# Spreading 32 DRAM-to-DRAM weight-sum transfers along the weight stream of an SSD and GLA kernel

## Chip, cores and metric

The kernel runs on one core of one Trainium2 chip. The metric is the device time of one execution in microseconds (us), as the median of several runs. The engines are TensorE (PE, with its weight loads shown apart as PEld), VectorE (DVE), ScalarE (ACT), GpSimd (POOL) and SyncE (SP); DMAs are issued from the queues of SP and POOL and run on the core's 16 DMA engines.

## The reference

Two layers of a residual network act on x of 512 tokens by 1024 features, each behind an RMS norm, with a last RMS norm at the end.

```
h = x
h = h + ssd_mixer(rmsnorm(h), ...)     # layer 1: 32 heads in 8 groups, scanned in both directions
h = h + gla_mixer(rmsnorm(h), ...)     # layer 2: 4 heads
return rmsnorm(h, final_norm)

def gla_mixer(u, w_in, ...):
    q, k, v, z, gl = split(u @ w_in)   # v and z: 4 heads of 512 columns each
    ...                                # decay from gl, attention in both directions, norm, times silu(z)
    return o @ w_out
```

The products are wanted in float32. Each weight is split into a high and a low part, and each product is made of three matmuls.

## The kernel before, in words

**The weight stream.** All weights go through one object, `Weights` (L46 to L113). A list of 146 specs names the tiles of 512 KB in the order of their use; `W.pos` counts the one in use. `W.next()` is called where the matmuls of a position are written. It splits ahead to position `pos + 2`, loads ahead to `pos + 2`, and hands out the parts. A load goes from SP's queue into one of three `wraw` buffers (L65). The split is a cast on ACT into `whi` (L85, or L90 in two halves where a column scale applies) and a subtraction on DVE into `wlo` (L86 or L91); there are three buffers of each. `W.mark` is the ACT instruction of the latest split. Positions 0 to 64 belong to the SSD layer (`n1` in the diff is 65), 65 to 145 to the GLA layer. A position is 24 matmuls, or 12 in the block products of GLA (`block_mm`, L801).

**The SSD layer.** The loop over g (L727) projects group g and runs the scan of group g - 1 in between, a part at each call of `step()` (L731). `scan_group` asks for two tiles `bct` of 1 MB from DRAM on POOL's queue (`load_bc`, L533); there are two buffers, which come free with the matmuls of `outputs` (L652). ACT adds biases to `bct` (L611), DVE selects (L616), ACT takes exponentials (L619), DVE multiplies (L620), PE multiplies (L652). Then `y` is gated (L662), squared on ACT (L666), its root taken on POOL (L303, L304), scaled on ACT (L669), and transposed on PE into `pty` (L677).

**The weight sums.** GLA's v and z of a head are computed with seven block products (`vz_part`) in place of eight, for which four sums w1 to w4 of blocks of `w_in` are needed. For each of the 4 heads `Blocks.step(n)` (L249) starts transfer n of 8 from DRAM to DRAM on POOL's queue, 1 MB each: n = 0, 1, 4 and 6 are copies (L264), n = 2, 3, 5 and 7 accumulate (L262), here called adds. Within a head n = 2 follows on n = 0, 3 on 1, 4 on 2, 5 on 4, 6 on 5 and 7 on 6. Each waits for `W.mark` by a manual dependency:

```
tc.add_manual_dep(dma.ins, W.mark.ins.name, ..., reason="pace")
```

The sums are read back as `wraw<-wsumw` at positions of the head's `vz_part`: from 72 for head 0, 88 for head 1, 108 for head 2, 128 for head 3. Before the change the list is ordered by n and then by head (L278), and each `step()` of the SSD loop with g of 1 or more starts the next (L732), so all 32 are started in groups 1 to 5.

**Order.** The instructions are ordered on each engine by a list scheduler that works with priorities and modelled times; an engine's queue then runs in that order, POOL's and SP's too. Tail parts at the end are ordered by hand (`manual_schedule`, L1094).

Of the kernel before, what the change touches and what calls it, by code (L numbers as in the profile page):

```python
# [45 lines left out]
class Weights:  # L46
    def __init__(self, tc, pool):
        self.tc, self.nc, self.pool = tc, tc.nc, pool
        self.specs = []
        self.alt = {}  # L50
        self.raw = {}
        self.spl = {}
        self.pos = 0
        self.n_raw = 0
        self.n_spl = 0

# [44 lines left out]
    def next(self):  # L101
        n = len(self.specs)
        while self.n_spl < n and self.n_spl <= self.pos + LOOK_SPL:
            while self.n_raw <= self.n_spl:
                self._load(self.n_raw)
                self.n_raw += 1
            with self.tc.high_priority(offset=SPLIT_AHEAD):
                self._split(self.n_spl)
            self.n_spl += 1
        self.load_ahead()  # L110
        i = self.pos
        self.pos += 1
        return self.spl.pop(i)  # L113


def build(tc, I, out):
    nc = tc.nc
    ctx = ExitStack()
    with ctx:
# [3 lines left out]
        W = Weights(tc, cp)  # L123
# [90 lines left out]
        def outw(w, r0, scale):  # L214
            for hf in range(2):
                for kk in range(2):
                    W.add(
                        w[r0 + kk * 256 : r0 + (kk + 1) * 256, hf * 512 : (hf + 1) * 512].rearrange(
                            "(k p) f -> p k f", p=P
                        ),  # L220
                        (2, 512),
                        scale=scale[:, kk * 2 : kk * 2 + 2],
                    )
# [14 lines left out]
        last1 = len(W.specs) - 1  # L238

        class Blocks:  # L240
# [8 lines left out]
            def step(self, n):  # L249
                w = self.w  # L250
                dst, src, add = (
                    (w["w1"], self.b11, False),
                    (w["w3"], self.b12, False),
                    (w["w1"], self.b12, True),
                    (w["w3"], self.b22, True),
                    (w["w2"], w["w1"], False),
                    (w["w2"], self.b22, True),
                    (w["w4"], w["w2"], False),
                    (w["w4"], self.b21, True),
                )[n]  # L260
                if add:
                    dma = nc.gpsimd.dma_start(dst, src, accum_op=ALU.add)  # L262
                else:
                    dma = nc.gpsimd.dma_start(dst, src)  # L264
                tc.add_manual_dep(
                    dma.ins, W.mark.ins.name,
                    mybir.DependencyInfo(mybir.DependencyClass.Sync, mybir.DependencyReason.DATA),
                    reason="pace",
                )
# [5 lines left out]
                        W.add(src[kk * 256 : (kk + 1) * 256].rearrange("(k p) f -> p k f", p=P), (2, 512))  # L275

        blocks = [Blocks(hd) for hd in range(GH)]
        sums = [(b, n) for n in range(8) for b in blocks]  # L278

        def qk_specs(hd):  # L280
            chan(w_in2, GQ0 + hd * P)
            chan(w_in2, GK0 + hd * P)
# [8 lines left out]
        for hd in range(GH):  # L291
# [3 lines left out]
            if hd + 1 < GH:  # L295
                qk_specs(hd + 1)
        outw(w_out2, 3 * 512, onT)

        uh = cp.tile([P, KD, L], F32R, name="uh")
        ul = cp.tile([P, KD, L], F32R, name="ul")  # L300
# [32 lines left out]
        def proj_tok(step=lambda: None):  # L333
            pts = [mmb(f"ptk{t}") for t in range(NT)]
            for kk in range(4):
                if kk:
                    step()
                wh, wl = W.next()
                for t in range(NT):
                    sl = slice(t * P, (t + 1) * P)  # L340
                    for j in range(2):
                        k = 2 * kk + j
                        mm3(pts[t], (uh[:, k, sl], ul[:, k, sl]), (wh[j], wl[j]), k == 0, k == KD - 1)
            return pts

        def proj_out(yts, step=lambda: None):
            for hf in range(2):
                pts = [mmb(f"po{t}") for t in range(NT)]
                for kk in range(2):
                    if hf or kk:  # L350
                        step()
                    wh, wl = W.next()
                    for t in range(NT):
                        for j in range(2):
                            k = 2 * kk + j
                            mm3(pts[t], yts(k, t), (wh[j], wl[j]), k == 0, k == 3)
                for t in range(NT):
                    hs = h[t][:, hf * 512 : (hf + 1) * 512]
                    nc.vector.tensor_tensor(out=hs, in0=hs, in1=pts[t], op=ALU.add)  # L359
# [27 lines left out]
        with tc.tile_pool(name="sp", bufs=1, reuse_waits="tile") as sp:  # L387
# [108 lines left out]
            def proj_group(g, step):  # L496
                b = conv_silu(proj_ch(), 16 + g, "bch")
                step()
                c = conv_silu(proj_ch(), 24 + g, "cch")
                step()  # L500
                x0 = conv_silu(proj_ch(), 2 * g, "xch")
                step()
                x1 = conv_silu(proj_ch(), 2 * g + 1, "xch")
                return b, c, x0, x1

            def z_gate(pts, pool, n):
                zs = []
                for t in range(NT):
                    if t % 2 == 0:
                        zs.append(pool.tile([P, 2, 512], F32, tag="zs", name=f"zs{t}", bufs=n))  # L510
                    z = zs[-1][:, t % 2]
                    nc.scalar.activation(z, pts[t], AF.Tanh, scale=0.5)
                    nc.vector.scalar_tensor_tensor(
                        out=z, in0=z, scalar=1.0, in1=pts[t], op0=ALU.add, op1=ALU.mult
                    )
                return zs
# [193 lines left out]
            def yts1(pr):  # L710
                def f(k, t):
                    yh, yl = yT[2 * pr + k // 2]
                    sl = slice(t * P, (t + 1) * P)
                    return yh[:, k % 2, sl], yl[:, k % 2, sl]

                return f
# [10 lines left out]
            for g in range(G + 1):  # L727
                it = iter(scan_group(g - 1, grp.pop(g - 1), zs[(g - 1) // 2])) if g else iter(())
                left = [SCAN_STEPS, 4 * ((g % 2 == 0 and g < G) + (g < G) + (g in (3, 5, 8)))]

                def step():  # L731
                    if g and sums:  # L732
                        b, i = sums.pop(0)
                        b.step(i)
                    n = -(-left[0] // max(left[1], 1))
                    left[0] -= n
                    left[1] -= 1
                    for _ in range(n):
                        next(it, None)

                if g < G:
                    if g % 2 == 0:
                        zs[g // 2] = z_gate(proj_tok(step), sp, 3)
                        step()
                    if g == 0:
                        dt_part()
                    grp[g] = proj_group(g, step)
                    step()
                if g in (3, 5, 8):
                    proj_out(yts1(g // 2 - 1 if g < 8 else 2), step)  # L750
                for _ in it:
                    pass
# [366 lines left out]
```

## Time and profile before

| what | value |
|---|---|
| median of 3 runs | 894.0 us (893.67 to 896.81) |
| the profiled execution | 896.26 us |
| its span, first to last instruction | 894.6 us |
| mean granted TensorE clock | 0.986 of full speed |
| PE busy | 847.1 us (95%) |
| DVE, ACT, POOL busy | 678.3, 512.7, 99.8 us |
| moved by DMA | 132.92 MB |

All times within the program are counted from the span's start. A row of a timeline gives start, duration and instruction, and in brackets the idle time of the engine before it and what ended it. A DMA's time to landing counts from its issue. What an engine is not kept from doing by another is busy time; only idle time of PE, and time at a lower PE clock, can be won without removing matmuls.

### The profile page before, as it was taken

How to read it: one execution, taken by the hardware profiler on the slowest of the kernel's cores; microseconds unless marked ns; L12 is line 12 of the kernel's file. 1: busy time of each engine (PE TensorE's matmuls, PEld its weight loads, DVE VectorE, ACT ScalarE, POOL GpSimd, SP SyncE). 2: the span in 40 equal slices, each digit the busy share in tenths (PEclk: the TensorE clock that was granted, in tenths of full speed). 3: DMA queues.
4: the chain of work that ended last, by engine and by line, in shares of the span. 5: the costliest groups of instructions: out<-in, count | busy, mean ns of one | idle time of the engine just before them, and what ended most of it. 6: DMA issues, size and time to landing. Idle time of an engine off the chain costs nothing.

```text
span 894.6 us, 11289 instructions
## 1 busy us (share of the span) xinstructions
PE 847.1 (95%) x3976; PEld 691.9 (77%) x3976; DVE 678.3 (76%) x1040; ACT 512.7 (57%) x1082; POOL 99.8 (11%) x172
## 2 busy tenths in 40 slices
PE   7999989979999999999898998999999999999996
PEld 5777778868887788888777776877887788778875
DVE  6398968789658987679698689878855886588653
ACT  6338478556546746567485548586525652575333
POOL 2002022111111110000001140000001000100012
PEclk9999999989999999999899999999999999999999
DMA  7337659998799794332222135513532363236202
GB/s 252 95 97 288 209 195 225 259 185 279 203 252 341 180 214 140 95 109 103 95 95 94 42 104 164 144 46 125 182 95 71 118 189 91 75 102 213 85 1 94
DMA packets 90198, 132.92 MB, mean 149 GB/s; under 512 B 7969, under 2 KB 49149, under 8 KB 87966
## 3 DMA queue, kind: packets, MB, share of 16 engines
q1 hardware_dynamic: 76412, 80.68, 30.0%
q0 software_dynamic: 13728, 51.52, 21.0%
q8 instruction: 31, 0.51, 0.2%
q14 instruction: 25, 0.20, 0.1%
q10 hardware_dynamic: 2, 0.00, 0.0%
HBM read 129.96 MB, written 35.78 MB: 185 GB/s over the span
## 4 chain that ended last, share of the span: by engine, by line
PE 60%; DVE 12%; ACT 10%; issue 7%; DMA 7%; POOL 3%; POOLq 0%; SPq 0%; ACTq 0%; DVEq 0%
DMA bct<-cumd 5%; PE pb L137 4%; PE pb L138 4%; PE pb L139 4%; PE pch L138 4%; PE pch L139 4%; PE pch L137 4%; PE po L137 4%; PE po L138 4%; PE po L139 4%; DVE wlo L86 2%; PE pyi L652 2%; PE ptk L139 2%; PE ptk L137 2%; PE ptk L138 2%
## 5 line engine op out<-in xcount | busy, mean ns | idle before, releaser
L85 ACT CAST whi<-wraw 128x1024 fp32r<-128x1024 f32 (+1 forms) x114 | 118.8, 1043 | 140.4 <-PE pb L139 40.5
L86 DVE TENSOR_TENSOR wlo<-wraw,whi 128x1024 fp32r<-128x1024 f32 (+1 forms) x114 | 140.4, 1233 | 76.9 <-ACT whi L85 76.5
L138 PE MATMUL pch<-ul,whi 128*128 128x512 f32 (+2 forms) x336 | 134.0, 399 | 0.0
L139 PE MATMUL pch<-uh,wlo 128*128 128x512 f32 (+2 forms) x336 | 133.3, 397 | 0.6 <-DVE wlo L86 0.5
L137 PE MATMUL pch<-uh,whi 128*128 128x512 f32 (+2 forms) x336 | 133.7, 398 | 0.0
L139 PEld LDWEIGHTS pch<-uh,wlo 128*128 128x128 f32 (+2 forms) x336 | 62.9, 187 | 15.1 <-DVE wlo L86 1.5
L137 PEld LDWEIGHTS pch<-uh,whi 128*128 128x128 f32 (+2 forms) x336 | 62.8, 187 | 13.9 <-issue 0.2
L138 PEld LDWEIGHTS pch<-ul,whi 128*128 128x128 f32 (+2 forms) x336 | 62.8, 187 | 13.9 <-issue 0.5
L488 DVE SCALAR_TENSOR_TENSOR cv<-pch,colA,cv 128x511 f32<-128x511 f32 (+1 forms) x96 | 70.9, 743 | 0.4
L90 ACT ACTIVATE whi<-wraw,colB 128x512 fp32r<-128x512 f32 x58 | 38.8, 716 | 44.5 <-PE pch L138 20.1
L611 ACT ACTIVATE bct<-bct,eb 128x128 f32<-128x128 f32 x128 | 41.5, 392 | 22.8 <-DMA bct<-cumd 19.5
L137 PE MATMUL ptk<-whi,uh 128*128 128x512 f32 x128 | 51.3, 403 | 0.0
L303 POOL TENSOR_SCALAR rs<-ss 128x2 f32<-128x2 f32 (+1 forms) x32 | 8.0, 250 | 386.7 <-ACT gy L1025 309.5
L139 PE MATMUL ptk<-whi,ul 128*128 128x512 f32 x128 | 50.8, 398 | 0.0
L138 PE MATMUL ptk<-wlo,uh 128*128 128x512 f32 x128 | 50.8, 397 | 0.0
L91 DVE SCALAR_TENSOR_TENSOR wlo<-wraw,colB,whi 128x512 fp32r<-128x512 f32 x58 | 41.7, 748 | 9.2 <-ACT whi L90 8.7
L619 ACT ACTIVATE bct<-bct,eb 128x128 f32<-128x128 f32 x128 | 41.3, 392 | 6.1 <-DVE bct L616 6.0
L137 PE MATMUL pb<-whi,uh 128*128 128x512 f32 x96 | 38.6, 402 | 2.0 <-DVE u L825 2.0
L137 PE MATMUL po<-whi,yh 128*128 128x512 f32 x96 | 38.7, 406 | 0.0
L138 PE MATMUL pb<-wlo,uh 128*128 128x512 f32 x96 | 38.6, 403 | 0.0
L359 DVE TENSOR_TENSOR h<-h,po 128x512 f32<-128x512 f32 x48 | 31.9, 683 | 8.8 <-PE po L139 8.7
L138 PE MATMUL po<-wlo,yh 128*128 128x512 f32 x96 | 38.4, 400 | 0.0
(306 smaller groups left out, 2050.1 us busy)
## 6 DMA issues: line engine op xcount, KB each, us to landing
wraw<-in_ssd_w_in_dram SPq DMA_DIRECT2D x48, 512.0 KB, 6.8
wsumw<-in_gla_w_in_dram POOLq DMA_DIRECT2D x24, 1024.0 KB, 11.0
bct<-cumd POOLq DMA_DIRECT2D x16, 1024.0 KB, 7.7
wraw<-in_gla_w_in_dram SPq DMA_DIRECT2D x32, 512.0 KB, 3.7
wraw<-wsumw SPq DMA_DIRECT2D x32, 512.0 KB, 3.5
wraw<-in_ssd_w_out_dram SPq DMA_DIRECT2D x16, 512.0 KB, 5.1
wraw<-in_gla_w_out_dram SPq DMA_DIRECT2D x16, 512.0 KB, 3.8
h<-in_x_dram SPq DMA_DIRECT2D x4, 512.0 KB, 6.5
```

Source lines behind the costliest of these rows:

```text
L85: self.mark = nc.scalar.copy(vh, raw)
L86: nc.vector.tensor_tensor(out=vl, in0=raw, in1=vh.bitcast(F32), op=ALU.subtract)
L90: self.mark = nc.scalar.mul(hs[j], raw[:, j], g)
L91: nc.vector.scalar_tensor_tensor(out=ls[j], in0=raw[:, j], scalar=g, in1=hs[j].bitcast(F32), op0=ALU.mult, op1=ALU.subtract)
L137: nc.tensor.matmul(pt, lhsT=a[0], rhs=b[0], start=first, stop=False)
L138: nc.tensor.matmul(pt, lhsT=a[0], rhs=b[1], start=False, stop=False)
L139: nc.tensor.matmul(pt, lhsT=a[1], rhs=b[0], start=False, stop=last)
L359: nc.vector.tensor_tensor(out=hs, in0=hs, in1=pts[t], op=ALU.add)
L488: nc.vector.scalar_tensor_tensor(out=cv[:, o0:o1], in0=pt[:, o0 + s : o1 + s], scalar=cwt(j, a), in1=cv[:, o0:o1], op0=ALU.mult, op1=ALU.add,)
L611: nc.scalar.activation(bct[:, r], bct[:, r], AF.Identity, bias=TM["eb"][:, cc, i : i + 1])
L619: nc.scalar.activation(et[:, r], et[:, r], AF.Exp, bias=TM["eb"][:, cc, i : i + 1])
L652: nc.tensor.matmul(py[:, q * 256 + r * 64 : q * 256 + (r + 1) * 64], lhsT=et[:, r], rhs=xt[:, cc, r * 64 : (r + 1) * 64], start=True, stop ...
```

## The change

The list of sums and its use in `step()` go. `W.next()` looks up its position in a table `W.beside` and runs what it finds, after the splits and loads ahead have been asked for. The table holds the 32 transfers, head by head and n = 0 to 7 within a head: 20 at positions 8, 10, 13, 16, 19, 21, 24, 27, 30, 32, 35, 38, 41, 43, 46, 49, 52, 54, 57 and 60 of the SSD layer, and 12 at positions 68, 73, 78, 83, 88, 92, 96, 100, 104, 108, 112 and 116, within the first three heads of GLA. So heads 0 and 1 are complete by position 49; the first four transfers of head 2 are at 52 to 60, its last four at 68 to 83; head 3 is at 88 to 116. The transfers, their sizes, queue and kind of wait are the same.

```
         self.pos = 0
+        self.beside = {}
...
         self.load_ahead()
         i = self.pos
+        self.beside.get(i, lambda: None)()
         self.pos += 1
...
         blocks = [Blocks(hd) for hd in range(GH)]
-        sums = [(b, n) for n in range(8) for b in blocks]
...
+        n1 = last1 + 1
+        at = [8 + (n1 - 10) * i // 20 for i in range(20)] + [n1 + i for i in (3, 8, 13, 18, 23, 27, 31, 35, 39, 43, 47, 51)]
+        for i, pos in enumerate(at):
+            W.beside[pos] = lambda b=blocks[i // 8], n=i % 8: b.step(n)
...
                 def step():
-                    if g and sums:
-                        b, i = sums.pop(0)
-                        b.step(i)
```

## Rows read from the trace of the kernel before

**Rows 1.** The page, busy time of each engine.
```profile
PE 847.1 (95%) x3976; PEld 691.9 (77%) x3976; DVE 678.3 (76%) x1040; ACT 512.7 (57%) x1082; POOL 99.8 (11%) x172
```

**Rows 2.** Busy time by stretch; the last three columns: PE clock, DMA share, GB/s.
```profile
69.00:190.00 121.00, 109.94 (x533) 91.06 (x534) 99.80 (x175) 83.89 (x216) 20.64 (x30) 0.96 0.84 238
190.00:335.00 145.00, 142.03 (x687) 117.72 (x687) 116.42 (x188) 84.94 (x208) 21.55 (x32) 1.00 0.90 236
335.00:428.00 93.00, 92.62 (x463) 77.28 (x462) 73.24 (x121) 59.27 (x146) 4.51 (x9) 1.00 0.35 109
428.00:500.00 72.00, 63.95 (x319) 52.94 (x318) 56.39 (x99) 43.04 (x120) 7.43 (x16) 0.95 0.27 88
```

**Rows 3.** DMA issues in 60 to 340 us: count, KB each, median us to landing.
```profile
wraw<-in_ssd_w_in_dram SPq DMA_DIRECT2D x28, 512.0 KB, 9.2
bct<-cumd POOLq DMA_DIRECT2D x11, 1024.0 KB, 8.9
```

**Rows 4.** DMA issues in 340 to 500 us.
```profile
bct<-cumd POOLq DMA_DIRECT2D x5, 1024.0 KB, 5.6
```

**Rows 5.** Timeline of PE, instructions that it came late to, 110 to 442 us.
```profile
112.98 0.48 PE L677 MATMUL pty<-idn,y 128*128 128x128 f32 x1 [2.76 <-ACT y L669]
...
182.53 0.98 PE L548 MATMUL ptx<-idn,cv 128*128 128x128 f32 x7 [3.33 <-DVE cv L493]
...
185.26 1.12 PE L553 MATMUL ptb<-idn,cv 128*128 128x128 f32 x4 [1.50 <-ACT xt L549]
...
285.32 0.70 PE L635 MATMUL pti<-st,cv 128*128 128x256 f32 x2 [1.31 <-DVE t L642]
...
303.50 0.66 PE L553 MATMUL ptb<-idn,cv 128*128 128x128 f32 x4 [0.93 <-ACT xt L549]
...
440.97 0.47 PE L677 MATMUL pty<-idn,y 128*128 128x128 f32 x1 [2.90 <-ACT y L669]
```

**Rows 6.** Busy time by stretch, as in group 2, around one stall.
```profile
179.00:192.00 13.00, 8.16 (x32) 6.33 (x31) 11.79 (x26) 8.30 (x19) 1.82 (x2) 0.74 1.10 233
```

**Rows 7.** Timeline of ACT, 155 to 438 us.
```profile
169.66 1.05 ACT L85 CAST whi<-wraw 128x1024 fp32r<-128x1024 f32 x1 [3.87 <-DMA wraw<-in_ssd_w_in_dram]
...
174.40 1.87 ACT L611 ACTIVATE bct<-bct,eb 128x128 f32<-128x128 f32 x6 [3.01 <-DMA bct<-cumd]
...
432.44 1.34 ACT L90 ACTIVATE whi<-wraw,colB 128x512 fp32r<-128x512 f32 x2 [6.55 <-PE pch L138]
...
437.81 0.69 ACT L611 ACTIVATE bct<-bct,eb 128x128 f32<-128x128 f32 x2 [3.37 <-DVE bct L616]
```

**Rows 8.** The chain that ended last, two loads on it: start, us.
```profile
102.49 7.50 DMA bct<-cumd
...
163.23 11.14 DMA bct<-cumd
```

**Rows 9.** DMA issues in 429.5 to 430 us.
```profile
bct<-cumd POOLq DMA_DIRECT2D x1, 1024.0 KB, 8.1
```

**Rows 10.** DMA issues in 312.5 to 316 us, a stream load beside one add.
```profile
wraw<-in_ssd_w_in_dram SPq DMA_DIRECT2D x1, 512.0 KB, 9.3
```

**Rows 11.** DMA issues in 204 to 205.5 us, a stream load beside one copy.
```profile
wraw<-in_ssd_w_in_dram SPq DMA_DIRECT2D x1, 512.0 KB, 6.8
```

**Rows 12.** DMA issues in 500 to 890 us.
```profile
wraw<-wsumw SPq DMA_DIRECT2D x32, 512.0 KB, 3.5
```

**Rows 13.** Timeline of ACT in the GLA layer.
```profile
545.12 1.06 ACT L85 CAST whi<-wraw 128x1024 fp32r<-128x1024 f32 x1
...
551.96 1.04 ACT L85 CAST whi<-wraw 128x1024 fp32r<-128x1024 f32 x1
...
627.05 1.05 ACT L85 CAST whi<-wraw 128x1024 fp32r<-128x1024 f32 x1 [1.67 <-PE pb L139]
```

**Rows 14.** Timeline of DVE in the GLA layer.
```profile
554.86 1.22 DVE L86 TENSOR_TENSOR wlo<-wraw,whi 128x1024 fp32r<-128x1024 f32 x1
...
628.14 1.23 DVE L86 TENSOR_TENSOR wlo<-wraw,whi 128x1024 fp32r<-128x1024 f32 x1 [1.50 <-ACT whi L85]
```

## Prediction, made before the change was run

> **What bounds the kernel now.** I read the page first: PE is busy for 847.1 us [rows 1], so matmuls set the time, and only the 47 us in which PE is idle, and the time at half clock, are open to a change that moves no matmul. Next comes the table by stretch [rows 2]. From 69 to 335 us, where all 32 transfers run, PE is idle for 121 - 109.94 + 145 - 142.03 = 14.0 us, and the DMA engines are 84 to 90% busy. From 335 to 428 us the same loop goes on with no transfer in it: PE is idle for 0.4 us, DMA is at 35%. From 428 us the scan of the last group has little left to cover it, and PE is idle for 8.1 us with no transfer near. The reader should see that crowding of DMA and idle PE stand together, but that the last stretch has a cause of its own.
>
> The DMA tables say what crowding costs a load: among the transfers a stream load lands after 9.2 us and a bct tile after 8.9 [rows 3]; later bct takes 5.6 [rows 4] and a stream load in GLA 3.5 [rows 12].
>
> Then the timelines, for how a late load reaches PE. Six waits make up 12.7 us, over half of the idle PE time between 69 and 500 us [rows 5]. Before the one at 182.53 us ACT sat idle twice, 3.87 us for a stream load and 3.01 us for a bct tile [rows 7], and the chain shows that tile landing 11.14 us after its issue [rows 8]. ACT runs in order, so the convolution work behind the tile came late, then DVE's, then PE's. The clock also fell: 0.74 over 13 us [rows 6] is 0.26 x 13 = 3.4 us lost between the full level and half. The stall at 112.98 has the same form: a bct tile issued at 102.49 lands at 109.99 [rows 8], and the squares of y stand behind it on ACT.
>
> **The change, part by part.** Nothing is removed: 32 issues of the same size stay on POOL, which is busy 11% [rows 1]. What changes is what each transfer runs beside. I placed the new transfers in the old time scale by the casts of ACT, one per position: a transfer at position p waits for the cast of p + 2. Some anchors: 23 is cast at 169.66 us, 59 at 432.44 [rows 7], 75 at 545.12 [rows 13]. In the SSD layer one transfer then starts about every 20 us (20 over some 400 us), where before there were 32 in about 260, one every 8.
>
> *Middle of SSD.* By this placement (an estimate) the transfers near 163 us are a copy at about 152 and an add at about 171, and the tile issued at 163.23 meets neither in full. In the old order, with one start every 8 us and landings of some 11, adds overlapped there all the time. I take the stall at 182.53 and 185.26 as gone: 3.33 + 1.50 [rows 5] + 3.4 of clock [rows 6] = 8.2 us. The two small waits at 285.32 and 303.50 follow on crowded loads too: 1.31 + 0.93 [rows 5] = 2.2 us gone. At 97 us an add now stands where a copy stood, and the tile of 102.49 still meets it: its 7.50 [rows 8] goes towards 8.9 [rows 3], so I add 1 us to that stall. Other waits I leave as they are. Part sum: -8.2 - 2.2 + 1.0 = -9.4 us. Bounds: nothing, if DVE (74 to 82% busy here, from [rows 2]) holds PE anyway; at most all 14.0 us idle and 0.04 x 121 = 4.8 us of clock [rows 2], -18.8.
>
> *End of SSD.* Four transfers now fall behind 380 us. The add at position 57 waits for the cast of 432.44 (until 433.8) [rows 7]; the tile issued at about 429.7 lands 8.1 us later [rows 9], at 437.8, when ACT goes on [rows 7], and PE waits 2.90 us at 440.97 [rows 5]. Beside an add that tile goes from 8.1 towards the 11.14 of a crowded one [rows 8]: 0 to 3.0 us, straight into the stall. I take +2. The add at position 60 comes near 459 us; the loads then are ahead of need, +0.
>
> POOL's queue runs in order, so what stands behind a waiting transfer matters: the bct issues, the roots of L303 and L304, and in GLA the same roots for the gate. Each transfer waits for a cast that comes two positions before use, so the wait seldom outlasts what is behind it. If the add of position 57 were ordered ahead of the tile of 429.7, the tile would leave about 4.5 us later (cast end 433.8, about 0.4 us more to issue); I keep this as an upper end.
>
> *GLA.* Twelve transfers are added to a layer that had none. A position here lasts 1.05 + 1.67 = 2.72 us [rows 13]. ACT's cast waits for PE (the split buffers), and the load three positions on leaves when DVE has split: 628.14 + 1.23 - 627.05 = 2.3 us after the cast starts [rows 13, 14]. A load thus has 3 x 2.72 - 2.3 = 5.9 us until its cast is due, and takes 3.5 [rows 12]: 2.4 us spare. A late cast in turn has 2 x 2.72 - 2.3 = 3.1 us before PE misses it. So an isolated load may take 5.9 + 3.1 = 9.0 us. Beside one copy a load took 6.8 us [rows 11]: hidden, +0, unless several follow each other. Beside one add it took 9.3 [rows 10]: 0.3 us too much, and the load after it stands in the same queue. I take 0.5 us for each of the adds at 96, 108 and 116: +1.5; bounds 0 and 9.3 - 5.9 = 3.4 each, if no split buffer is ahead.
>
> Head 0 is tighter. The add of position 73 leaves after the cast that ends at 546.2 [rows 13]. The load cast at 551.96 left about 547.5 (the split of three positions earlier); beside the add it lands near 556.8, cast end 557.8, where DVE wanted it at 554.86 [rows 14]: 2.9 us late on an engine that has no idle time there. I take 2.5; bounds 0 and 2.9. The adds of 83 and 100 fall where positions are twice as long: +0. The first transfer of this part, at 68, meets no tight load: +0.
>
> **Sum.** -9.4 + 2.0 + 1.5 + 2.5 = -3.4 us. The profiled execution took 896.26 us, 1.7 around its span of 894.6: 892.9 on its scale. It lies 2.3 above the median of 894.0, so on the median I forecast 890.6. Measurement of this kernel can tell about 0.5%, 4.5 us, from no change; the forecast lies just inside.
>
> **The rivals.**
>
> 1. *The sum above*: the middle of SSD is freed, the tail and GLA give about two thirds back. 890.6; own range 886 to 895. Chance 0.48 (0.19 of it faster, 0.29 the same).
>
> 2. *Nothing is given back.* The split buffers hide every add, the tail's tile lands before the add has moved much: 894.0 - 9.4 = 884.6, and down to 894.0 - 18.8 = 875 if all idle time of the stretch goes. For it: the load tolerance of 9.0 us is nearly what a load beside an add takes. Against: head 0 has no such reserve. Chance 0.20, faster.
>
> 3. *The spreading frees nothing.* A tile meets a transfer in the new places as often as not, and each stall is DVE's in the end: middle of SSD 0, the other terms +6: 894 to 900. For it: DVE is 74 to 82% busy, and the stall's own release is DVE's [rows 5]. Against: 93 us without transfers and without idle PE [rows 2]. Chance 0.16 (0.12 the same, 0.04 slower).
>
> 4. *Slower: GLA's weight stream falls behind.* Three raw buffers give 2.4 us spare; four adds in block products (73, 96, 108, 116) at the full 3.4 us, and four copies (78, 88, 92, 112) at 6.8 - 5.9 = 0.9 us, come to 17.2. With the tail and the SSD gain: 894.0 - 9.4 + 2.0 + 17.2 = 903.8. It decides from where GLA loses 9.4 - 2.0 + 4.5 = 11.9 us, seven tenths of that. For it: 9.3 against 3.5 us [rows 10, 12]. Against: the split buffers. Chance 0.16 (0.15 slower, 0.01 the same). The Trainium skill, in "DMA: Bandwidth & Descriptors", section "Issuing engines are not separate DMA queues", says that DMAs of all issuing engines share the same 16 DMA engines and interleave; by that rule a transfer on POOL's queue slows SP's loads wherever it is put, and the trace agrees in size, 9.3 against 3.5 us.
>
> That the change starts fewer or other transfers is excluded: the table has 32.
>
> **How the numbers follow.** Faster 0.19 + 0.20 = 0.39; the same 0.29 + 0.12 + 0.01 = 0.42; slower 0.04 + 0.15 = 0.19. The range leaves out the far half of rivals 2 and 4: 881 to 902.
>
> **What would show it.** Right: from 130 to 335 us PE idle under 2 us and no half clock near 185; bct tiles at 6 to 7.5 us in the median; the last bct tile but one at 10 us and a longer wait before `pty` in the tail; a longer PE wait in head 0's block products; stream loads of 7 to 9 us in GLA beside adds, with PE waits under 1 us. Wrong: stalls of the 182 kind that come back elsewhere in SSD (rival 3), or casts in GLA that wait for DMA for several us (rival 4); or a scheduler that orders ACT, DVE or POOL anew because modelled transfer times moved.

## The result: slower by 0.9%, and where the time went

The changed kernel takes 900.68 us in the median (900.16 to 904.0, 4 runs), against 894.37 for the kernel before, run beside it: a ratio on record of 1.0093, 95% interval 1.0065 to 1.0121; the two medians alone give 1.0071. The forecast was a small gain, 890.6; measured is a loss, 6.3 us by the medians. The profiled execution took 900.56 us with a span of 898.9, so the two profiled spans differ by 4.3 us, and the time can be placed by them. Lines of the code have moved down by 1 to 6: L677 of before is L683 after, L85 is L86, L359 is L365, L262 is L264.

The table by stretch, the changed kernel, columns as in [rows 2]:

```profile
69.00:190.00 121.00, 113.72 (x560) 95.10 (x561) 103.44 (x181) 87.37 (x225) 12.39 (x20) 0.97 0.56 161
190.00:335.00 145.00, 144.12 (x711) 120.17 (x710) 118.34 (x192) 87.43 (x218) 15.35 (x24) 1.00 0.61 170
335.00:428.00 93.00, 92.34 (x457) 77.13 (x456) 75.43 (x127) 55.31 (x132) 9.06 (x14) 1.00 0.54 161
428.00:500.00 72.00, 59.62 (x291) 48.74 (x289) 49.45 (x87) 43.62 (x123) 8.91 (x19) 0.93 0.36 94
500.00:890.00 390.00, 371.32 (x1685) 301.77 (x1686) 282.65 (x391) 204.64 (x327) 43.16 (x63) 0.99 0.49 141
```

Against [rows 2] the DMA share of the first two stretches falls from 0.84 and 0.90 to 0.56 and 0.61, and PE idles 121 - 113.72 + 145 - 144.12 = 8.2 us there in place of 14.0. The loads there land sooner, DMA issues in 60 to 340 us as in [rows 3]:

```profile
wraw<-in_ssd_w_in_dram SPq DMA_DIRECT2D x30, 512.0 KB, 5.4
bct<-cumd POOLq DMA_DIRECT2D x12, 1024.0 KB, 7.4
```

So the middle of the SSD layer was relieved. From 428 to 500 us PE idles 12.4 us in place of 8.1. Over 500 to 890 us PE is busy for 371.32; the same stretch of the kernel before reads

```profile
500.00:890.00 390.00, 375.69 (x1710) 305.24 (x1708) 286.03 (x396) 208.78 (x336) 35.77 (x57) 1.00 0.36 109
```

To place the loss I compare the start of the same PE instruction in both. PE's timeline before, for instructions that [rows 5] lacks:

```profile
129.22 0.33 PE L677 MATMUL pty<-idn,y 128*128 128x128 f32 x1 [1.44 <-ACT y L669]
...
478.51 0.50 PE L137 MATMUL pr<-thw,yh 128*128 128x512 f32 x1 [1.91 <-DVE h L359]
...
497.19 0.66 PE L321 MATMUL ptn<-idn,xn 128*128 128x128 f32 x4 [0.60 <-DVE ul L143]
...
690.41 0.66 PE L1013 MATMUL ptyg<-idn,gy 128*128 128x128 f32 x4 [0.76 <-DVE gy L1027]
...
781.25 0.66 PE L1013 MATMUL ptyg<-idn,gy 128*128 128x128 f32 x4 [0.76 <-DVE gy L1027]
```

and the same instructions after, with the one long wait in head 0 (559.39) between them:

```profile
113.50 0.47 PE L683 MATMUL pty<-idn,y 128*128 128x128 f32 x1 [5.63 <-ACT y L675]
130.73 0.33 PE L683 MATMUL pty<-idn,y 128*128 128x128 f32 x1 [1.65 <-ACT y L675]
...
431.09 0.33 PE L683 MATMUL pty<-idn,y 128*128 128x128 f32 x1 [2.40 <-ACT y L675]
...
471.76 0.80 PE L139 MATMUL pr<-thw,yh 128*128 128x512 f32 x1 [6.79 <-DVE h L365]
...
492.93 0.66 PE L327 MATMUL ptn<-idn,xn 128*128 128x128 f32 x4 [1.18 <-DVE ul L145]
...
559.39 0.77 PE L139 MATMUL pb<-whi,uh 128*128 128x512 f32 x1 [5.83 <-DVE u L828]
...
691.67 0.55 PE L1016 MATMUL ptyg<-idn,gy 128*128 128x128 f32 x3 [0.76 <-DVE gy L1030]
...
785.59 0.66 PE L1016 MATMUL ptyg<-idn,gy 128*128 128x128 f32 x4 [0.76 <-DVE gy L1030]
```

The wait of 112.98 in [rows 5] begins at 112.98 - 2.76 = 110.22, after at 113.50 - 5.63 = 107.87: 2.4 us gained up to there. By 130.73 (129.22 before) 1.5 us are lost: the stall between cost 3.9. By the wait of 431.09 (440.97 in [rows 5]; both less their wait, 428.69 and 438.07) 9.4 us are gained. By 492.93 it is 4.3: the tail gave back 5.1. By 691.67 there is a loss of 1.3: head 0 cost 5.5 (head 1 hardly adds). By 785.59 it is 4.3: head 2 cost 3.1. Nothing more follows; 4.3 is the difference of the spans.

**The stall at 113 us.** DMA issues of POOL in 95 to 100.5 us, after:

```profile
wsumw<-in_gla_w_in_dram POOLq DMA_DIRECT2D x1, 1024.0 KB, 11.8
bct<-cumd POOLq DMA_DIRECT2D x1, 1024.0 KB, 9.9
```

The add at position 13 stands where a copy stood, as foretold. The tile behind it lands after 9.9 us in place of 7.50 [rows 8], and PE waits 5.63 in place of 2.76.

**The tail.** The add of position 60 leaves POOL at 458.39 us, and SP issues the next stream load 0.8 us later. Timelines of POOL, ACT and DVE there, and under them the chain of waits:

```profile
458.39 1.12 POOL L264 DMA_DIRECT2D wsumw<-in_gla_w_in_dram  x1 [11.26 <-ACT whi L91]
...
467.61 1.04 ACT L86 CAST whi<-wraw 128x1024 fp32r<-128x1024 f32 x1 [7.39 <-DMA wraw<-in_gla_w_in_dram]
...
468.68 1.23 DVE L87 TENSOR_TENSOR wlo<-wraw,whi 128x1024 fp32r<-128x1024 f32 x1 [3.83 <-ACT whi L86]
```
```profile
459.18 8.35 DMA wraw<-in_gla_w_in_dram
```

The load brings position 65, the first weights of the GLA layer, which PE uses much later. But its split stands in ACT's and DVE's order ahead of work of the tail: `h` (L365) is behind `wlo` (L87) on DVE, and the PE wait of 471.76 is for `h`. The kernel before had three of its four `h` behind that split too (DVE: `wlo` at 475.43, `h` from 477.78). So a load of which PE has no need yet holds up PE through two queues.

**Head 0.** The add of position 73 leaves at 543.08. Timelines of ACT and DVE, then the chain:

```profile
553.73 1.04 ACT L86 CAST whi<-wraw 128x1024 fp32r<-128x1024 f32 x1 [5.16 <-DMA wraw<-wsumw]
...
554.81 1.23 DVE L87 TENSOR_TENSOR wlo<-wraw,whi 128x1024 fp32r<-128x1024 f32 x1 [3.36 <-ACT whi L86]
```
```profile
546.91 9.33 DMA wraw<-wsumw
```

Two loads in a row are late beside one add: the first lands for the cast of 553.73, and DVE, which had no idle time at this point before [rows 14], stands 3.36 us. The second, issued at 546.91, takes 9.33 us, and the chain runs through it to `u` (L828) and to the PE wait of 559.39.

**The clock.** Three stretches of the changed kernel after its long waits, columns as in [rows 2]:

```profile
108.00:118.00 10.00, 4.50 (x13) 3.67 (x14) 5.06 (x9) 7.31 (x25) 0.91 (x2) 0.66 0.07 22
...
469.00:478.00 9.00, 6.24 (x27) 5.26 (x28) 5.84 (x9) 5.83 (x21) 0.90 (x2) 0.62 0.41 133
556.00:566.00 10.00, 6.61 (x18) 5.29 (x19) 7.76 (x14) 5.05 (x8) 0.52 (x1) 0.66 0.81 244
```

Each of the three waits of 5.6 to 6.8 us is followed by time at half clock: 0.34 x 10 or 0.38 x 9 = 3.4 us lost between the full level and half. Before, the first and the last of these places read 0.83 over 10 us (1.7 lost), and the one in the tail 1.00.

### The profile page after: what moved, and what is told of

Read it like the earlier page. It is cut to its first block, busy times and chain, and to the rows that moved or that the text cites. A ratio compares the mean times of both kernels' runs of the same rounds, so it can differ in the third digit from the quotient of the medians.

```text
span 898.9 us, 11292 instructions
## 1 busy us (share of the span) xinstructions
PE 845.4 (94%) x3976; PEld 691.1 (77%) x3976; DVE 677.8 (75%) x1040; ACT 513.1 (57%) x1082; POOL 100.8 (11%) x172
## 4 chain that ended last, share of the span: by engine, by line
PE 29%; DVE 7%; ACT 5%; DMA 5%; issue 2%; POOL 2%; POOLq 0%; SPq 0%; ACTq 0%; DVEq 0%
PE pb L139 3%; PE pb L140 3%; PE pb L141 3%; PE po L141 2%; PE po L139 2%; PE po L140 2%; DMA wraw<-wsumw 2%; DMA wraw<-in_gla_w_in_dram 2%; DVE wlo L87 1%; PE pch L140 1%; PE pch L139 1%; PE pch L141 1%; ACT whi L86 1%; PE pr L141 1%; PE pr L140 1%
## 5 line engine op out<-in xcount | busy, mean ns | idle before, releaser
L87 DVE TENSOR_TENSOR wlo<-wraw,whi 128x1024 fp32r<-128x1024 f32 (+1 forms) x114 | 140.4, 1234 | 86.1 <-ACT whi L86 85.7
L86 ACT CAST whi<-wraw 128x1024 fp32r<-128x1024 f32 (+1 forms) x114 | 118.8, 1043 | 149.8 <-PE pch L140 42.3
L139 PEld LDWEIGHTS pch<-uh,whi 128*128 128x128 f32 (+2 forms) x336 | 62.5, 186 | 13.6
L365 DVE TENSOR_TENSOR h<-h,po 128x512 f32<-128x512 f32 x48 | 32.0, 683 | 9.0 <-PE po L141 9.0
L141 PE MATMUL pb<-whi,ul 128*128 128x512 f32 x96 | 38.4, 400 | 0.0
L141 PE MATMUL po<-whi,yl 128*128 128x512 f32 x96 | 38.1, 397 | 0.0
## 6 DMA issues: line engine op xcount, KB each, us to landing
wsumw<-in_gla_w_in_dram POOLq DMA_DIRECT2D x24, 1024.0 KB, 10.4
```

The costliest lines, as they stand in the source:

```text
L86: self.mark = nc.scalar.copy(vh, raw)
L87: nc.vector.tensor_tensor(out=vl, in0=raw, in1=vh.bitcast(F32), op=ALU.subtract)
L139: nc.tensor.matmul(pt, lhsT=a[0], rhs=b[0], start=first, stop=False)
L141: nc.tensor.matmul(pt, lhsT=a[1], rhs=b[0], start=False, stop=last)
```

## The experiments

Ratios are to the kernel before, run on the same chip, with 95% intervals, as they stand on record; they need not be the quotients of the medians, and a difference of two ratios is known to 0.3 to 0.6%. Sizes in us are such differences times 894. In experiments 1 to 4 and 7 to 10 the traces show PE's matmuls in the changed kernel's order. In the diffs only the places in the list `at` are shown. "GLA transfers" are the twelve at positions 68 to 116.

**1. No transfers in GLA.** The last 12 transfers are left out, and the loads of the sums that are then missing (two of head 2, all four of head 3) read a weight block instead.

```
-        for i, pos in enumerate(at):
+        for i, pos in enumerate(at[:20]):
```

> This kernel leaves out the 12 transfers of the GLA layer; loads of head 2 (w2, w4) and of head 3 (w1 to w4) read a block of the weights instead, so the loads are as many and as large. The instruction order on PE, DVE, ACT is the changed kernel's. Theory (adds beside loads that are due just in time cost the GLA layer about 9 us: 6 in head 0, 3 in head 2): 900.7 - 9 = 891.7 us, ratio to before 0.997, and the PE wait at 553.6 us falls from 5.7 to about 2 us. Rival (the GLA loss is something that the SSD part carries over, such as order or an earlier start): 899 to 901, the PE wait stays over 5 us.

Measured: 888.16 us, 0.9941 (0.9921 to 0.9961). The GLA half of the change costs 1.0093 - 0.9941 = 1.5%, 13.6 us, so the SSD half alone is a gain. That is more than the 9 us expected and than the 8.6 that the trace places in heads 0 and 2. The tail's wait stays, 7.02 us at 469.62; that of head 0 falls to 2.02.

**2. The tail's add alone moved.**

```
-... 54, 57, 60, 68, 73, ...
+... 54, 57, 82, 68, 73, ...
```

> One transfer moved: the add of position 60 goes to position 82, between GLA heads 0 and 1, where the next load has some 20 us in hand. Theory (that add stands in front of the first GLA load, whose cast holds up ACT and DVE in order at 460 to 468 us): 900.7 - 4.6 = 896 us, ratio to before 1.002, the PE wait of 6.8 us near 465 falls to about 2 us and the load of position 65 lands in 4 us instead of 8.4. Rival (the tail is slower because its instruction order changed): 900 to 901, the wait stays over 5 us, since the order is kept but for two instructions.

Measured: 896.27 us, 1.0042 (1.002 to 1.0065): 0.5%, 4.6 us, from one transfer (the interval touches that of the changed kernel, so the size is rough). The wait for `h` falls to 2.88 us; that of head 0 stays, 6.12.

**3. The GLA transfers moved.** All twelve run, at other positions, outside the block products.

```
-... 68, 73, 78, 83, 88, 92, 96, 100, 104, 108, 112, 116
+... 68, 82, 84, 98, 100, 102, 103, 105, 118, 119, 121, 123
```

> All 12 GLA transfers stay in GLA but move from the block products to the stretches of query, key and output products between heads: positions 68, 82, 84, 98 (head 2) and 100, 102, 103, 105, 118, 119, 121, 123 (head 3). Theory (place, not number, costs): the GLA loss of 9 us goes as when they are left out, 892 us, ratio 0.997. Rival (12 MB more traffic in GLA costs wherever it runs): 897 to 901.

Measured: 889.43 us, 0.9965 (0.9946 to 0.9985). PE's timeline at head 0, where the wait of 5.83 stood:

```profile
554.47 0.47 PE L139 MATMUL pb<-whi,uh 128*128 128x512 f32 x1 [0.54 <-DVE u L828]
```

The same twelve transfers cost nearly nothing here: 0.9965 against 0.9941 without them, which is inside the noise. What costs is the place; by this experiment the old places cost 1.0093 - 0.9965 = 1.3%, 11.4 us.

**4. Both, and position 13 moved to 12.** The moves of 2 and 3 together (here 60 goes to 83), and the add ahead of the tile of the 113 us stall one position earlier.

```
-... 10, 13, 16, ... 57, 60, 68, 73, ...
+... 10, 12, 16, ... 57, 83, 68, 82, ...
```

> The GLA places of the third kernel, the add of position 60 at 83, and the add of position 13 at 12, so that it starts some 9 us earlier and is done before the bct tile of about 100 us is asked for. Theory: 900.7 - 9 (GLA) - 4.6 (tail) - 4 (the 5.6 us wait and half clock near 108 us) = 883 us, ratio 0.988; the wait near 108 us falls to 1.5 us or less. Rival (that early wait is DVE's, not the tile's): 887, the wait stays over 4 us.

Measured: 881.82 us, 0.9872 (0.985 to 0.9893), faster than both kernels: by 1.3% than before, by 2.2% than the change. PE's timeline at the three places:

```profile
109.88 0.33 PE L683 MATMUL pty<-idn,y 128*128 128x128 f32 x1 [1.90 <-ACT y L675]
...
461.98 0.77 PE L139 MATMUL pr<-thw,yh 128*128 128x512 f32 x1 [2.88 <-DVE h L365]
...
545.65 0.47 PE L139 MATMUL pb<-whi,uh 128*128 128x512 f32 x1 [2.05 <-DVE u L828]
```

The waits of 5.63, 6.79 and 5.83 us are back at 1.9 to 2.9. Of the 2.2%, experiment 2 explains 0.5 and experiment 3 1.3; the 0.4 that are left, 3.8 us, are the size of the stall at 113 (3.9 above). That move was not run by itself, but up to this point in time no other transfer has been moved, and the wait there is 3.7 us shorter.

**5 and 6. The transfers nearly without traffic**, in the old order and in the new: each transfer moves 16 of its 512 rows, and the loads of the sums read a weight block.

```
+                dst, src = dst[0:16], src[0:16]
```

> The kernel before, with each of the 32 transfers cut to its first 16 of 512 rows (32 KB in place of 1 MB), and the weight loads of the sums reading a block of the weights instead. The instruction order of PE, DVE, ACT is exactly that of before. Theory (before the change, traffic of the transfers cost what PE lost between 69 and 335 us): the 14.0 us of idle PE there fall to 4 or less and the half clocks there go; 12 to 16 us faster than before, ratio 0.983 to 0.987. Rival (those waits are DVE's or the order's): 1 to 5 us faster, ratio 0.995 to 0.999.

Measured, kernel before cut in this way: 880.46 us, 0.9871 (0.9833 to 0.991). Between 69 and 335 us PE still idles 7.0 us, more than the 4 expected.

> The changed kernel, cut in the same way; its instruction order of PE, DVE, ACT is exactly the changed kernel's. Theory (order is worth little, traffic all): within 3 us of the fifth kernel, ratio to before 0.982 to 0.988, which makes the changed kernel's transfers cost about 20 us where they stand and those of before about 14. Rival (part of the loss is the new order): slower than the fifth kernel by 4 us or more, ratio over 0.989.

Measured, changed kernel cut in this way: 881.2 us, 0.9888 (0.9839 to 0.9936). In both the instructions stand in the order of the full kernel. So the two orders are worth the same within the noise, and the difference is the traffic: it cost 1.3% in the old places and 1.0093 - 0.9888 = 2.0% in the new. The profiled spans agree: 894.6 - 881.1 = 13.5 us in the old, 898.9 - 880.2 = 18.7 in the new. Experiment 4, at 0.9872 with all its traffic and a span of 879.5, pays about nothing for it.

**7. Head 0's places alone.**

```
-... 60, 68, 73, 78, 83, 88, ...
+... 60, 68, 82, 83, 84, 88, ...
```

> The changed kernel with head 0's three transfers moved behind its block products: 73 to 82, 78 to 83, 83 to 84; the other nine of GLA stay. Theory: the wait of 5.7 us and the half clock near 553 us go, 6 us of the changed kernel's loss: ratio to before 1.002 to 1.004. Rival (the transfers in the block products of heads 1 and 2 carry most of the GLA loss): ratio 1.006 to 1.009.

Measured: 895.35 us, 1.0041 (1.0011 to 1.0071), 0.5% or 4.6 us from head 0, with intervals that overlap; its wait is 2.03.

**8. One add put back at 73** into experiment 3.

```
-... 60, 68, 82, 84, 98, ...
+... 60, 68, 73, 84, 98, ...
```

> The third kernel (GLA transfers between the heads), with one add put back from position 82 to 73, within head 0's block products. Theory: the PE wait near 550 us comes back at about 5.7 us with 6.8 us at half clock: 6 us slower than the third kernel, ratio to before about 1.003. Rival (one transfer is absorbed, only a row of them costs): 0 to 2 us, ratio 0.997 to 0.999.

Measured: 895.51 us, 1.0037 (1.0013 to 1.0061): 0.7%, 6.4 us, for one transfer in this place. DMA issues around it, and PE's timeline:

```profile
wsumw<-in_gla_w_in_dram POOLq DMA_DIRECT2D x1, 1024.0 KB, 13.4
wraw<-wsumw SPq DMA_DIRECT2D x1, 512.0 KB, 9.7
```
```profile
557.16 0.76 PE L139 MATMUL pb<-whi,uh 128*128 128x512 f32 x1 [6.34 <-DVE u L828]
```

**9. A copy in that place.** The copy of position 68 goes to 73 in experiment 3; is it the adding that makes the load late?

```
-... 60, 68, 82, 84, ...
+... 60, 73, 82, 84, ...
```

> The third kernel, with a copy in that place instead (position 68 to 73). By the rows of before a load beside a copy takes 6.8 us where 5.9 are to be had, so in theory 0 to 2 us slower than the third kernel, ratio 0.997 to 0.999, and a PE wait under 3 us there. Rival (any transfer in that place costs the same, because the latency of the meeting decides and not its bytes): 5 to 6 us slower, ratio about 1.003.

Measured: 892.39 us, 0.9998 (0.9978 to 1.0019). DMA issues, and PE's timeline:

```profile
wraw<-wsumw SPq DMA_DIRECT2D x1, 512.0 KB, 9.3
wsumw<-wsumw POOLq DMA_DIRECT2D x1, 7.6
```
```profile
553.88 0.77 PE L139 MATMUL pb<-whi,uh 128*128 128x512 f32 x1 [5.18 <-DVE u L828]
```

The theory that a copy is cheap falls: its load lands as late as beside an add, though the copy itself is done in 7.6 us and the add in 13.4.

**10. A copy out of the weights in that place.** Its source rows are short, as the adds' are, where those of experiment 9 are long; position 100 goes to 73.

```
-... 84, 98, 100, 102, ...
+... 84, 98, 73, 102, ...
```

> The third kernel, with a copy at position 73 that reads a block of the weights (rows of 2 KB) in place of the ninth kernel's copy from sum to sum, which went out as 16 rows of 64 KB and held the load beside it for 9.3 us. Theory (packets of 64 KB hold an engine's turn so long that the load waits as behind an add): here the load lands after 6 to 7 us, the PE wait is under 3 us, ratio to before 0.996 to 0.998. Rival (any 1 MB transfer in that place costs the same): the load lands after 9 us, wait of 5 us, ratio 1.000 or more.

Measured: 895.09 us, 1.0034 (1.0008 to 1.006). The theory on the size of the packets falls too; the same two views:

```profile
wsumw<-in_gla_w_in_dram POOLq DMA_DIRECT2D x1, 1024.0 KB, 9.4
wraw<-wsumw SPq DMA_DIRECT2D x1, 512.0 KB, 8.6
```
```profile
555.29 0.77 PE L139 MATMUL pb<-whi,uh 128*128 128x512 f32 x1 [4.44 <-DVE u L828]
```

In that place any of the three costs 4.4 to 6.3 us of waiting and 0.3 to 0.7%. The intervals of 9 and 10 overlap, and the wait of 10 is shorter while its time is longer, so which copy is the dearer stays open.

**11. All 32 spread evenly over the SSD layer.**

```
+        at = [8 + 52 * i // 32 for i in range(32)]
```

> All 32 transfers spread over the SSD layer, head by head, at positions 8 to 58 (about one in 1.6 positions); none in GLA, none after 58. Theory (traffic in SSD costs when loads meet several transfers at once; the tail and GLA are free of them): between the two, ratio 0.990 to 0.996, PE idle of 69 to 428 us between 4 and 14 us. Rival (density hardly matters in SSD, only the last places did): as the fourth kernel, ratio 0.985 to 0.989.

Measured: 898.87 us, 1.0071 (1.0039 to 1.0102). Both the theory and its rival missed: a kernel that spreads the transfers more evenly than before, and has none in GLA, is slower than before. The scheduler had also ordered many instructions anew, so two causes were left.

**12. The same order without the traffic.** The cut of 5 and 6, on 11.

> The run with all 32 transfers in the SSD layer, evenly spread, with each transfer cut from 512 rows to 16 (32 KB moved in place of 1 MB) and the four sums read from a block of the weights, so the stream's loads stay and only the traffic of the transfers is left out; the order of the instructions is that run's. Traffic theory (that run's 1.007 of the kernel before is what its transfers do to the loads they run beside): the same 0.987 to 0.989 as the two cut kernels before, with the waits at 83, 110, 180, 353 and 434 us gone. Rival (the new order of the scheduler is what made that run slow): 0.995 or more, with those waits still there though nothing moves beside them.

Measured: 879.28 us, 0.9842 (0.9819 to 0.9865). Table by stretch of 11, then of 12, columns as in [rows 2]:

```profile
69.00:190.00 121.00, 113.02 (x556) 93.72 (x555) 102.30 (x179) 85.68 (x224) 15.37 (x23) 0.99 0.69 196
...
335.00:428.00 93.00, 89.42 (x445) 74.69 (x444) 71.97 (x121) 53.63 (x129) 12.85 (x19) 1.00 0.77 211
428.00:500.00 72.00, 59.65 (x292) 48.83 (x291) 51.60 (x91) 42.49 (x120) 7.84 (x16) 0.95 0.34 95
```
```profile
69.00:190.00 121.00, 117.36 (x590) 97.97 (x589) 108.89 (x189) 87.56 (x226) 14.91 (x25) 1.00 0.40 125
...
335.00:428.00 93.00, 91.13 (x456) 76.02 (x456) 74.87 (x125) 57.84 (x144) 9.91 (x16) 1.00 0.36 108
428.00:500.00 72.00, 64.41 (x314) 52.27 (x313) 54.85 (x94) 42.25 (x110) 10.46 (x21) 0.95 0.25 72
```

The order is not slow (it came out a little faster than the range expected); the traffic in it costs 1.0071 - 0.9842 = 2.3%, more than the 1.3% that the kernel before pays. Where it is lost, the start of one PE instruction at the end of the SSD layer tells: first in experiment 5, where it is the instruction of 440.97 in [rows 5], then in 11 and 12:

```profile
428.97 0.33 PE L678 MATMUL pty<-idn,y 128*128 128x128 f32 x1 [3.03 <-ACT y L670]
```
```profile
436.45 0.33 PE L683 MATMUL pty<-idn,y 128*128 128x128 f32 x1 [2.54 <-ACT y L675]
```
```profile
423.90 0.33 PE L684 MATMUL pty<-idn,y 128*128 128x128 f32 x1 [1.36 <-ACT y L676]
```

Each less its wait, the traffic has cost (440.97 - 2.90) - (428.97 - 3.03) = 12.1 us up to here in the kernel before, and (436.45 - 2.54) - (423.90 - 1.36) = 11.4 in experiment 11. So up to the end of the SSD layer the 32 transfers cost about the same close together, at a DMA share of 0.84 to 0.90 in the two stretches where they run, and evenly spread, at 0.69 to 0.77. The excess of 11 lies behind this point: of the differences of the spans, 13.5 and 894.1 - 877.7 = 16.4, 1.4 us are left there in the kernel before and 5.0 in experiment 11. Its last add starts at 447.45 us, and the chain shows the load issued 1.1 us later, for which ACT waits 4.10 us:

```profile
448.54 8.96 DMA wraw<-in_ssd_w_out_dram
```

PE waits 3.63 us at 466.44 for `xchw`, which stands behind that load's split on ACT. So this is a loss of the same form as in the changed kernel's tail. The two traces are single executions, that of 11 the fastest of its runs.

## Why the prediction was wrong

**The middle of the SSD layer was right, sum and all.** Foretold was -9.4 us, and 9.4 us are gained up to the wait of 431.09. The stalls from 182 to 303 us are gone, for which the prediction took -8.2 - 2.2 = -10.4; measured from 130.73 on is 9.4 + 1.5 = 10.9. The stall at 113 was seen, and mis-sized: +1.0 stood for a tile that lands 1.4 us later, measured is 3.9 us. The tile came 2.4 us later, PE waited 2.9 us longer, and the half clock behind the wait cost 3.4 us where it had cost 1.7, of which the term had nothing. What stood there before was hardly the transfers' doing: with their traffic cut (experiment 5) the tile still lands after 7.4 us and PE waits 2.69, only without the half clock behind it. That the whole agrees is luck in this part: 2.4 us were gained ahead of 108 us, where nothing was foretold. Of the signs named for it, PE idle from 130 to 335 us (1.6 us), the full clock near 185 us and the bct tiles (7.4 us) came as foretold; the longer wait before `pty` in the tail did not.

**The first step that failed is "The add at position 60 comes near 459 us; the loads then are ahead of need, +0".** No row stood behind it. In the kernel before the load in question was issued at 469.94 us and landed after 3.8; its cast began at 474.35, so it was ahead by some 0.6 us, and beside the add it takes 8.35. "Need" was also judged by PE, where it has to be judged by ACT's and DVE's order, in which this split stands ahead of the tail's own work. Experiment 2 gives the price, 4.6 us, by moving this one transfer. About 1 us of the tail's 5.1 seems to be the new order: the wait for `h` is 2.88 us also in experiment 6, without the traffic, where it was 1.91 before. The +2 was put on the add of position 57 instead, which left at 425.03 us, 4.5 us after its tile was issued; that tile landed after 7.3 us, sooner than the 8.1 of [rows 9], with a PE wait of 2.40 in place of 2.90, and less time at half clock behind it (1.7 us lost, 0.86 over 12 us from 428, where it was 3.4): no loss there against the kernel before.

**The second is the size of head 0.** Place and mechanism held: the split comes 3.36 us late on DVE, foretold 2.9. But 2.9 was given as the upper bound, and head 0 cost 5.5 us by the trace, 4.6 by experiment 7, and 6.4 for the one add of experiment 8. Two things were missing: the second load in the queue is late as well (9.33 us, on the chain), and PE's wait is followed by half clock, which cost 1.7 us more than before.

**The other block products** cost 3.1 us in place of 1.5, within the bounds, and all in head 2: the add at 108 lets ACT wait 5.14 us for a load at 719.87, and the copy at 112 4.00 us for one at 731.94. That a load beside one copy is hidden, at 6.8 us, rested on too mild a row: experiments 9 and 10 measure 9.3 and 8.6. The copies at 88 and 92 and the add at 96, in head 1, cost nothing that can be seen: PE is 1.3 us late at 598 us and still at 691. So some transfers in block products are hidden, as rival 2 had it.

**The sum.** Tail 5.1 - 2.0 = 3.1 too low, head 0 3.0, the rest of GLA 1.6: together 7.7, from -3.4 to the +4.3 of the two profiled executions. The medians lie 2.0 further apart, since the profiled execution of before lay 1.9 above its median.

**The rivals.** Rival 4 had the sign. Its mechanism is half of the cause: GLA's stream does fall behind, by 8.6 us in the trace, 5.5 of them in one place; the tail did the rest. Whether it passed the 11.9 us from which it was to decide stays open, since experiments 1 and 3 put the GLA loss at 13.6 and 11.4. Its rule that a transfer slows SP's loads wherever it is put says little of the time: experiment 4 starts all 32 and loses next to nothing by them. Rival 3 falls: the SSD half alone is a gain of 0.6% (experiment 1), with the tail's loss still in it. Rival 2, nothing given back, wasn't this kernel; experiment 4 comes near it, 881.8 us, where the rival said 884.6.

**What a load pays.** The DMA queues of the changed kernel from 462.6 to 467.5 us, while the load of position 65 and the add both move; q0 is POOL's, q1 SP's; packets, MB, share of the 16 engines:

```profile
q0 software_dynamic: 305, 0.62, 72.8%
q1 hardware_dynamic: 286, 0.55, 35.8%
```

Both queues move about as many packets, and each of POOL's takes about twice as long: 0.728 x 16 x 4.9 / 305 = 0.19 us against 0.10. The shares add up to 109%, so packets of the two overlap in part. A reading that fits is that the load waits for one of the slow packets ahead of each of its own. The Trainium skill says in "DMA: Bandwidth & Descriptors", section "Queues, rings and completion order", that each DMA engine goes round the queues that have work and takes a whole packet from one before it turns to the next. The equal counts, 305 against 286, agree with that if a packet of the page is a packet of the profile, which the trace doesn't show; nor does it show in what order one engine took them. Experiment 9 limits the reading. POOL's queue there, from 537 to 550 us:

```profile
q0 software_dynamic: 32, 1.05, 24.0%
```

Sixteen of these 32 carry the data, 64 KB each, for about 0.240 x 16 x 13 / 16 = 3.1 us, and yet the load beside them lands 5.5 us later than the 3.8 of a load alone. So equal turns may explain the adds; why the copies cost as much stays open. What is shown goes without the rule: it matters little how busy the engines are on average (12.1 and 11.4 us lost at shares of 0.84 to 0.90 and 0.69 to 0.77, experiments 5, 11 and 12), and much whether a load that someone waits for is issued while a transfer of the other queue moves (experiments 2, 3, 4 and 8). That adds and copies are alike in this was measured in one place only.

**Left open.** A deeper weight stream (a fourth raw buffer) would test whether more lead takes away the stalls of the tail and of head 0; it wasn't tried. Which loads experiment 11's transfers met was followed for the last of them alone.

## What to carry to other kernels

A background transfer is not priced by how busy the DMA engines are but by the loads issued in the few microseconds behind its start (0.8 to 4.7 us in the stalls followed here): for each start, look up which load that is, and what stands behind its consumer in the order of its engine, also where PE has no need of the data yet. Here 13 starts out of 32 in other places (experiment 4) made 2.2% of the time. A stall is to be priced with the clock behind it: 3.4 us after each of the three long ones here.

## What the runs showed of the hardware that was not expected

- A load of 512 KB that lands in 3.5 to 3.8 us alone took 8.3 to 9.7 behind the start of a 1 MB transfer from DRAM to DRAM. In the one place where all three kinds were run it was 9.7 behind an add, 9.3 behind a copy with long rows and 8.6 behind one with short rows, although the three themselves land in 13.4, 7.6 and 9.4 us.
- Up to the end of the SSD layer the 32 transfers cost about the same spread evenly (11.4 us at a DMA share of 0.69 to 0.77) as close together (12.1 us at 0.84 to 0.90).
- Each PE wait of 5.6 to 6.8 us in the changed kernel was followed by a stretch at half clock (1.2 of 2.4 GHz) that cost 3.4 us. After shorter waits it ranged from nothing (1.91 us, at 478.51 before) over 1.7 (2.76, at 112.98) to 3.4 (2.90, at 440.97, 0.72 over 12 us).
